# The second mixer's weight tiles are split during the first MLP and kept in DRAM as high and low parts

## The chip, the cores and the metric

The kernel runs on one core of a Trainium2 chip. The time is the device time of one execution in microseconds (us); lower is better. The engines are TensorE (PE, with PEld for its weight loads), VectorE (DVE), ScalarE (ACT), GpSimd (POOL) and SyncE (SP). SP and ScalarE each have a queue from which DMAs are issued.

## The reference

Two decoder layers on 528 tokens (16 meta tokens and 512 of input), width 1024, all in float32:

```python
for l in range(DEPTH):                       # DEPTH = 2
    a = rmsnorm(h, mix_pre_g[l])
    proj = a @ w_in[l]                       # 1024 x 2304: q, k, v, b_gate, c_gate, hc
    q, k = partial_rope(q, cos, sin), partial_rope(k, cos, sin)
    y_attn = sliding_window_gqa_sinks(q, k, v, sinks[l])
    y_conv = short_gated_conv(b_gate, c_gate, hc, conv_w[l])
    y = concat(rmsnorm(y_attn, ...), rmsnorm(y_conv, ...))
    h = h + rmsnorm(y @ w_out[l], mix_post_g[l])
    a = rmsnorm(h, mlp_pre_g[l])
    f = square(relu(a @ w_up[l])) @ w_down[l]   # 1024 -> 4096 -> 1024
    h = h + rmsnorm(f, mlp_post_g[l])
return h[:, N_META:]
```

## The kernel before

Activations stand transposed: 128 partitions of the feature dimension, 8 blocks `k`, 528 tokens in two ranges (272 and 256). Each float32 operand is split into a high part, rounded to `F32R`, and a low part, the rest. A product is three matmuls, hi·hi, hi·lo and lo·hi (`mm3`, lines 195 to 198), so a gemm of one weight tile (1024 x 128) with one range is 8 x 3 = 24 matmuls into one of eight PSUM banks.

A weight tile is loaded in two halves of 128 x 512 into `wraw` (five buffers) by SP's queue. `cast` (line 106) splits a half: ScalarE writes the high part (line 107), VectorE subtracts it from the raw half (line 108). `blocks` (line 80) lists all weight tiles in the order in which they are used: for each layer the two tiles of k and v, four of q, twelve of the gates and the convolution's input, eight of `w_out`, then in four chunks the tiles of `w_up` and `w_down`. `prep` (line 134) loads and splits the next block into two tiles of the tag `w`, which has 14 slots: seven tiles ahead (`CAP`), five in part of the mixer (`PCAP`). `tile_done` frees a tile after its last gemm and prepares the next. In chunks 1 to 3 the up projections run in pairs of tiles (`fast_pair`) with seven products in place of eight; their sums of weight blocks (lines 123 to 130) are made by VectorE.

The Mixer (`mixer`) projects, swaps halves for rope by four small DMAs per range and tile (lines 558 and 559, to rows of `z`), and runs attention in 128-token blocks between the gemms: scores (line 653), softmax (line 629), transposes (line 684) and the product with v (line 202). Sums of squares for the norms are taken by a matmul with a matrix of ones (line 235). `boundary` ends a sub-layer: norms and residual for the first range stand beside the last gemms of the second, then `first_tiles` runs the first five tiles of the next sub-layer.

The MLP (`mlp`) takes chunk after chunk: eight up tiles, then eight down tiles; `one` runs one tile's gemms over both ranges. In chunk 0 five up tiles run in `first_tiles` and three through `one`, and in the last chunk two down tiles go through `one` and six are shared with `boundary`.

The instructions are issued by a scheduler when the program is built: it puts each engine's instructions into a fixed order, taking what is ready by its own model of time, in the program's order where several are. On the chip each engine follows its order and waits on semaphores.

Of the kernel before, what the change touches and what calls it, by code (L numbers as in the profile page):

```python
# [8 lines left out]
F32 = mybir.dt.float32  # L9
F32R = mybir.dt.float32r  # L10
# [3 lines left out]
P = 128  # L14
# [22 lines left out]
def trunk_kernel(ctx, tc, xT, gains, sinkb, sinkm, rope, masks, maskm, ident_in, w_in, w_out, w_up, w_down, outT):  # L37
    nc = tc.nc
    ACT, DVE, POOL, PE = nc.scalar, nc.vector, nc.gpsimd, nc.tensor
# [3 lines left out]
    cp = ctx.enter_context(tc.tile_pool(name="cp", bufs=1))  # L43
# [33 lines left out]

    epst = cp.tile([P, 4], F32, name="epst")

    blocks = []  # L80
    for l in range(2):
        blocks += [("in", l, 512), ("in", l, 640)]
# [13 lines left out]
    prepared = []  # L96
    last_load = []
# [5 lines left out]
    def half():  # L103
        return wp.tile([P, 4, P], F32, tag="wraw", name="wraw", bufs=5)

    def cast(raw, hi, lo):
        ACT.activation(hi, raw, AF.Copy)  # L107
        DVE.tensor_tensor(lo, raw, hi.bitcast(F32), ALU.subtract)  # L108
# [4 lines left out]
    def prep_pair(l, m, n):  # L113

        if n == 0:
            for name, k, mm in (("A11", 0, m), ("A21", 0, m + 1), ("A22", 4, m + 1), ("A12", 4, m)):
                pair[name] = half()
                nc.sync.dma_start(pair[name], w_up[l].rearrange("(k p) m -> p k m", p=P)[:, k:k + 4, P * mm:P * mm + P])
        flat = lambda t: t.rearrange("p k m -> p (k m)")
        f = wp.tile([P, KT, P], F32R, tag="w", name="wf", bufs=2 * CAP)  # L120
        if n == 1:
            pair["S1"], pair["S2"] = (utile()[:, :512].rearrange("p (k m) -> p k m", k=4) for _ in range(2))
            DVE.tensor_tensor(pair["S1"], pair["A21"], pair["A22"], ALU.add)
            DVE.tensor_tensor(pair["S2"], pair["A11"], pair["S1"], ALU.subtract)
        if n == 2:
            pair["S3"] = pair["A21"]
            DVE.tensor_tensor(pair["S3"], pair["A21"], pair["A11"], ALU.subtract)
        if n == 6:
            pair["S4"] = pair["S2"]
            DVE.tensor_tensor(pair["S4"], pair["A12"], pair["S2"], ALU.add)  # L130
        cast(pair[("A11", "S2", "S3", "S1", "A12", "A22", "S4")[n]], f[:, 0:4, :], f[:, 4:8, :])
        prepared.append((f[:, 0:4, :], f[:, 4:8, :]))

    def prep(beside=None):

        if len(prepared) == len(blocks):
            return
        taken[0] += size(len(prepared))
        kind, l, sub = blocks[len(prepared)]
        if kind == "upx":  # L140
            return prep_pair(l, *sub)
        hi = wp.tile([P, KT, P], F32R, tag="w", name="whi", bufs=2 * CAP)
        lo = wp.tile([P, KT, P], F32R, tag="w", name="wlo", bufs=2 * CAP)
        raws = []
        for i in range(2):
            raw = half()
            raws.append(raw)
            ks = slice(4 * i, 4 * i + 4)
            dma = nc.sync.dma_start
            if kind == "out":  # L150
                col = slice(P * sub, P * sub + P)
                if i == 0:
                    for g in range(2):
                        dma(raw[g * 64:(g + 1) * 64], w_out[l, g * 256:(g + 1) * 256, col].rearrange("(j p) m -> p j m", p=64))
                else:
                    dma(raw, w_out[l, 512:1024, col].rearrange("(k p) m -> p k m", p=P))
            elif kind == "q":
                for g in range(2):
                    last_load[:] = [dma(raw[:, :, 64 * g:64 * g + 64], w_in[l].rearrange("(k p) m -> p k m", p=P)[
                        :, ks, 256 * g + 64 * sub:256 * g + 64 * sub + 64])]  # L160
            elif kind == "down":
                c, m = sub
                dma(raw, w_down[l, c * 1024:(c + 1) * 1024, P * m:P * m + P].rearrange("(k p) m -> p k m", p=P)[:, ks, :])
            else:
                src, off = (w_in, sub) if kind == "in" else (w_up, P * sub)
                last_load[:] = [dma(raw, src[l].rearrange("(k p) m -> p k m", p=P)[:, ks, off:off + P])]
            if beside:

                beside[2 * i]()
                cast(raw, hi[:, ks, :], lo[:, ks, :])  # L170
                beside[2 * i + 1]()
        if not beside:
            for i in range(2):
                ks = slice(4 * i, 4 * i + 4)
                cast(raws[i], hi[:, ks, :], lo[:, ks, :])
        prepared.append((hi, lo))

    def wtile():
        used[0] += 1
        return used[0] - 1  # L180

    def wtiles(n):
        return [wtile() for _ in range(n)]

    def refill(most=9):
        while len(prepared) < len(blocks) and taken[0] + size(len(prepared)) <= 2 * cap[0] and most:
            prep()
            most -= 1

    def tile_done(most=9):  # L190
        taken[0] -= size(done[0])
        done[0] += 1
        refill(most)
# [10 lines left out]
    def mms(items, act, hooks={}):  # L204


        banks = [bank() for _ in items]
        items = [(prepared[w], r, ev) for w, r, ev in items]
        for k in range(KT):
            ahi, alo = act(k)  # L210
            for (w, (t0, t1), _), ps in zip(items, banks):
                mm3(ps[:, :t1 - t0], w[0][:, k, :], w[1][:, k, :], ahi[:, t0:t1], alo[:, t0:t1], k == 0, k == KT - 1)
            if k in hooks:
                hooks[k]()
        return [lambda ev=ev, ps=ps, n=t1 - t0: ev(ps[:, :n]) for (_, (t0, t1), ev), ps in zip(items, banks)]

    def gemm(item, act):
        for ev in mms([item], act):
            ev()
# [47 lines left out]
    def new_acc(name):  # L267
        accs[name] = tp.tile([P, L], F32, tag="acc", name="acc", bufs=2)
        held.discard(name)
# [228 lines left out]
    def xrange(l):  # L498
        return (RA if l == 0 else XA, RB)
# [395 lines left out]
    def f_evac(m, r):  # L895
        t0, t1 = r

        def ev(ps):
            f = tmp(t1 - t0) if t1 - t0 <= 272 else utile()[:, :t1 - t0]
            DVE.tensor_scalar(f, ps, 0.0, None, ALU.max)  # L900
            ACT.activation(f, f, AF.Square)
            split(f_hi[:, m, t0:t1], f_lo[:, m, t0:t1], f)
        return ev
# [80 lines left out]
    def mlp(l, nxt, first):  # L984

        xr = xrange(l)

        full = xr if l == 0 else [(xr[0][0], xr[1][1])]

        def one(evac, act):  # L990
            w = wtile()
            for r in full:
                gemm((w, r, evac(r)), act)
            tile_done()

        txs[l] = [wp.tile([P, 4, L // 2], F32R, tag="x", name="tx", bufs=3) for _ in range(3)]
        for c in range(NCH):
            if c == 0:
                for m in range(NA, 8):
                    one(lambda r: f_evac(m, r), act_a)  # L1000
            else:
                for m in range(0, 8, 2):
                    fast_pair(l, m)
            last = c == NCH - 1
            if last:
                new_acc("h")
            for m in range(2 if last else 8):
                one(lambda r: z_evac(m, r, c > 0, last, (l, G_MPOST)), act_f)
                if c == 0 and m < 4:
                    fast_sums(l, m)  # L1010
        if nxt is not None:
            clear_pad()
        w = wtiles(6)
        for m in range(6):
            gemm((w[m], xr[0], z_evac(2 + m, xr[0], True, True, (l, G_MPOST))), act_f)
        boundary(l, w, act_f, G_MPOST, lambda r: Post(l, G_MPOST, r, nxt), first)

    def clear_pad():
        POOL.memset(kk[:, :, :PAD].bitcast(F32), 0.0)

    m0, m1 = Mixer(0), Mixer(1)
    first = [(m.items, m.tables, PCAP, "c") for m in (m0, m1)]
    sA, sB = Start(0, 0, RA, (0, 0)), Start(0, 0, RB, (0, 0))
    prep((lambda: sA.load(0), lambda: sA.steps(0), lambda: sA.load(1), lambda: sA.steps(1)))
    prep((lambda: sA.load(2), lambda: sA.steps(2), lambda: sA.load(3), lambda: sA.steps(3)))
    for i in range(4):
        prep()
# [12 lines left out]
    first_tiles(act_a, sB, RA, RB, first[0])  # L1040
    mixer(0, m0, mlp_items(0))
    mlp(0, (1, G_PRE), first[1])
    mixer(1, m1, mlp_items(1))
    mlp(1, None, None)


# [57 lines left out]
```

## Time and profile before

| | us |
|---|---|
| median of 3 runs | 1097.63 (1096.83 to 1098.42) |
| the profiled execution | 1097.51 |
| its span, first to last instruction | 1095.7 |
| TensorE busy | 1074.3 |
| VectorE busy | 801.3 |
| ScalarE busy | 624.6 |
| bytes read from and written to HBM | 97.88 MB, 2.10 MB |

In the profile a group of instructions is named by line, engine, operation and tile (`wlo<-wraw,whi` writes wlo from wraw and whi). The granted clock of TensorE was 0.996 over the span. In the profiled execution the first mixer runs up to about 200 us, the first MLP from 214 to 540 us, the boundary and the second mixer from 540 to about 750 us, and the second MLP from there to the end.

### The profile page before, as it was taken

The page shows a single profiled execution, that of the slowest core. Times are in us where ns is not written, and L with a number is a line of the kernel's source. Part 1 is how long each engine was busy: PE and PEld are TensorE (multiplying, and loading weights), DVE is VectorE, ACT ScalarE, POOL GpSimd, SP SyncE. Part 2 cuts the span into 40 slices and gives each one's busy share as a digit, 9 for nine tenths or more (in the row PEclk, how much of TensorE's full clock was granted, in tenths as well). Part 3 has the DMA queues.
Part 4 walks back from the last instruction along what each step waited for, and adds up shares of the span by engine and source line. Part 5 has one row for each costly group of instructions (what it writes and reads, how often), then busy time and mean ns, then how long its engine had stood idle before and what let it go on. Part 6 is the DMA issues. An engine that isn't in the chain of part 4 may idle for free.

```text
span 1095.7 us, 21642 instructions
## 1 busy us (share of the span) xinstructions
PE 1074.3 (98%) x8196; PEld 1030.8 (94%) x8196; DVE 801.3 (73%) x1895; ACT 624.6 (57%) x1510; POOL 10.8 (1%) x44
## 2 busy tenths in 40 slices
PE   8999999999999999999999999999999999999995
PEld 8999999999999999999989999999889989989995
DVE  7797886977585586586597988779947757757735
ACT  7576766665472383275365676667636625725732
POOL 2000000000000000000000000000000000000000
PEclk9999999999999999999999999999999999999998
DMA  9252122252252243144141412232422522522402
GB/s 249 64 146 59 58 78 79 77 155 59 69 152 85 59 127 110 49 124 137 26 112 39 130 58 59 78 97 82 130 72 84 154 68 79 162 68 71 143 1 77
DMA packets 206057, 102.06 MB, mean 93 GB/s; under 512 B 24000, under 2 KB 205904, under 8 KB 205952
## 3 DMA queue, kind: packets, MB, share of 16 engines
q1 hardware_dynamic: 205088, 99.89, 31.9%
q8 instruction: 64, 1.05, 0.4%
q10 hardware_dynamic: 688, 0.58, 0.2%
q14 instruction: 41, 0.34, 0.1%
q0 software_dynamic: 176, 0.21, 0.1%
HBM read 97.88 MB, written 2.10 MB: 91 GB/s over the span
## 4 chain that ended last, share of the span: by engine, by line
PE 88%; DVE 7%; ACT 1%; DMA 1%; issue 1%; SPq 1%; DVEq 0%; ACTq 0%
PE ps L196 28%; PE ps L198 28%; PE ps L197 28%; PE ps L202 1%; PE ps L684 1%; PE ps L653 1%; DVE wlo L108 1%; DVE a_lo L338 1%; DVE h L327 1%; DVE acc L280 1%; PE ps L235 1%; DMA h<-in_xT 0%; DVE t L326 0%; DMA z<-t 0%; SPq L558 0%
## 5 line engine op out<-in xcount | busy, mean ns | idle before, releaser
L197 PE MATMUL ps<-f_lo,whi 128*128 128x256 f32 (+2 forms) x1072 | 326.1, 305 | 0.0
L198 PE MATMUL ps<-f_hi,wlo 128*128 128x256 f32 (+2 forms) x1072 | 325.5, 305 | 0.0
L196 PE MATMUL ps<-f_hi,whi 128*128 128x256 f32 (+2 forms) x1072 | 322.9, 306 | 0.0
L197 PE MATMUL ps<-a_lo,whi 128*128 128x256 f32 (+3 forms) x808 | 230.2, 289 | 2.0 <-DVE a_lo L338 1.7
L196 PE MATMUL ps<-a_hi,whi 128*128 128x256 f32 (+3 forms) x808 | 227.2, 294 | 4.8 <-ACT a_hi L380 1.9
L198 PE MATMUL ps<-a_hi,wlo 128*128 128x256 f32 (+3 forms) x808 | 229.2, 288 | 0.1
L108 DVE TENSOR_TENSOR wlo<-wraw,whi 128x512 fp32r<-128x512 f32 x264 | 174.2, 688 | 51.8 <-ACT whi L107 31.5
L198 PEld LDWEIGHTS ps<-f_hi,wlo 128*128 128x128 f32 x1072 | 202.1, 189 | 9.1
L197 PEld LDWEIGHTS ps<-f_lo,whi 128*128 128x128 f32 x1072 | 201.6, 188 | 9.5
L107 ACT ACTIVATE whi<-wraw 128x512 fp32r<-128x512 f32 x264 | 153.9, 624 | 95.4 <-PE ps L197 58.4
L196 PEld LDWEIGHTS ps<-f_hi,whi 128*128 128x128 f32 x1072 | 199.5, 188 | 9.4
L196 PEld LDWEIGHTS ps<-a_hi,whi 128*128 128x128 f32 x808 | 148.1, 189 | 9.9 <-ACT a_hi L380 2.3
L197 PEld LDWEIGHTS ps<-a_lo,whi 128*128 128x128 f32 x808 | 152.6, 189 | 5.0 <-DVE a_lo L338 2.6
L198 PEld LDWEIGHTS ps<-a_hi,wlo 128*128 128x128 f32 x808 | 152.9, 189 | 1.4 <-DVE wlo L108 0.3
L510 DVE TENSOR_TENSOR z<-z,ps 128x272 f32<-128x272 f32 (+2 forms) x78 | 38.0, 487 | 99.9 <-PE ps L198 99.8
L107 ACT ACTIVATE wf<-wraw 128x512 fp32r<-128x512 f32 x96 | 59.7, 626 | 85.4 <-PE ps L197 51.8
L197 PE MATMUL ps<-a_lo,wf 128*128 128x264 f32 (+1 forms) x384 | 108.0, 282 | 0.0
L196 PE MATMUL ps<-a_hi,wf 128*128 128x264 f32 (+1 forms) x384 | 107.8, 282 | 0.0
L198 PE MATMUL ps<-a_hi,wf 128*128 128x264 f32 (+1 forms) x384 | 107.1, 283 | 0.0
L107 ACT ACTIVATE wf<-u 128x512 fp32r<-128x512 f32 x72 | 45.1, 627 | 88.4 <-PE ps L197 73.6
L108 DVE TENSOR_TENSOR wf<-wraw,wf 128x512 fp32r<-128x512 f32 x96 | 65.7, 688 | 11.5 <-ACT wf L107 10.5
L197 PEld LDWEIGHTS ps<-a_lo,wf 128*128 128x128 f32 x384 | 72.2, 188 | 0.1
(158 smaller groups left out, 1776.5 us busy)
## 6 DMA issues: line engine op xcount, KB each, us to landing
wraw<-in_w_up SPq DMA_DIRECT2D x128, 256.0 KB
wraw<-in_w_down SPq DMA_DIRECT2D x128, 256.0 KB
wraw<-in_w_in SPq DMA_DIRECT2D x56, 256.0 KB
wraw<-in_w_in SPq DMA_DIRECT2D x32, 128.0 KB
wraw<-in_w_out SPq DMA_DIRECT2D x32, 128.0 KB
wraw<-in_w_out SPq DMA_DIRECT2D x16, 256.0 KB
h<-in_xT SPq DMA_DIRECT2D x4, 272.0 KB
h<-in_xT SPq DMA_DIRECT2D x4, 256.0 KB
```

Source lines behind the costliest of these rows:

```text
L107: ACT.activation(hi, raw, AF.Copy)
L108: DVE.tensor_tensor(lo, raw, hi.bitcast(F32), ALU.subtract)
L196: PE.matmul(ps, whi, ahi, start=first, stop=False, skip_group_check=onto)
L197: PE.matmul(ps, whi, alo, start=False, stop=False, skip_group_check=onto)
L198: PE.matmul(ps, wlo, ahi, start=False, stop=last, skip_group_check=onto)
L202: PE.matmul(ps, a[n], b[n], start=first and n == 0, stop=last and n == 1)
L235: PE.matmul(ps, ones[:, which, :], acc, start=True, stop=more is None)
L280: return (eng or DVE).tensor_tensor(acc, acc, sq, ALU.add)
L327: DVE.tensor_tensor(hk, hk, t, ALU.add)
L338: DVE.scalar_tensor_tensor(a_lo[:, k, t0:t1], hk, g, a_hi[:, k, t0:t1].bitcast(F32), ALU.mult, ALU.subtract)
L510: DVE.tensor_tensor(zz, zz, ps, ALU.add)
L653: PE.matmul(outs[g], q[a][rows], k[b][rows], start=n == 0, stop=n == 2)
```

## The change

Two tiles are added, `sr` (a raw half) and `sf` (its high and low part), with one buffer each, and a pool `dp` in DRAM. In the first MLP, `one` calls `stash` after each gemm. A stash splits the half in `sr` into `sf`, stores `sf` to a DRAM tile of its own (128 x 2 x 512 words) and loads the next raw half into `sr`; both DMAs are issued on ScalarE's queue. `to_stash` has the 52 halves of the second layer's 26 tiles of `w_in` and `w_out`. `one` runs 29 tiles with two gemms each in the first MLP (three up, 26 down), so there are 58 calls, of which 52 do something. For a tile that is in `stashed`, `prep` issues four loads on SP's queue from DRAM straight into `hi` and `lo`; it uses no `wraw` and no `cast`. The loads of raw halves are moved into a function, `load_half`, unchanged.

```diff
+    sr = cp.tile([P, 4, P], F32, name="sr")
+    sf = cp.tile([P, 2, 4, P], F32R, name="sf")
+    dp = ctx.enter_context(tc.tile_pool(name="dp", bufs=1, space=bass.MemoryType.DRAM))
...
+    stashed = {}
+    to_stash = [(b, i) for b in blocks if b[1] == 1 and b[0] in ("in", "q", "out") for i in range(2)]
+
+    def stash():
+        if not to_stash:
+            return
+        (kind, l, sub), i = to_stash.pop(0)
+        cast(sr, sf[:, 0], sf[:, 1])
+        t = dp.tile([P, 2, 4, P], F32R, name=f"st_{kind}_{sub}_{i}")
+        ACT.dma_start(t.bitcast(F32), sf.bitcast(F32))
+        stashed.setdefault((kind, l, sub), []).append(t)
+        stash_load()
+
+    def stash_load():
+        if to_stash:
+            block, i = to_stash[0]
+            load_half(ACT, sr, *block, i)
...
     def prep(beside=None):
...
+        if (kind, l, sub) in stashed:
+            src = stashed[(kind, l, sub)]
+            for n, t in enumerate((hi, lo)):
+                for i in range(2):
+                    nc.sync.dma_start(t[:, 4 * i:4 * i + 4, :].bitcast(F32), src[i][:, n].bitcast(F32))
+            prepared.append((hi, lo))
+            return
...
             for r in full:
                 gemm((w, r, evac(r)), act)
+                if l == 0:
+                    stash()
             tile_done()
 
+        if l == 0:
+            stash_load()
         txs[l] = [wp.tile([P, 4, L // 2], F32R, tag="x", name="tx", bufs=3) for _ in range(3)]
```

More of the change, by code (lines that the diff above doesn't have):

```diff
@@ L132, in prep_pair, with load_half @@
         prepared.append((f[:, 0:4, :], f[:, 4:8, :]))
+    def load_half(queue, raw, kind, l, sub, i):
+        ks = slice(4 * i, 4 * i + 4)
+        dma = queue.dma_start
+        if kind == "out":
+            col = slice(P * sub, P * sub + P)
+            if i == 0:
+                for g in range(2):
+                    dma(raw[g * 64:(g + 1) * 64], w_out[l, g * 256:(g + 1) * 256, col].rearrange("(j p) m -> p j m", p=64))
+            else:
+                dma(raw, w_out[l, 512:1024, col].rearrange("(k p) m -> p k m", p=P))
+        elif kind == "q":
+            for g in range(2):
+                last_load[:] = [dma(raw[:, :, 64 * g:64 * g + 64], w_in[l].rearrange("(k p) m -> p k m", p=P)[
+                    :, ks, 256 * g + 64 * sub:256 * g + 64 * sub + 64])]
+        elif kind == "down":
+            c, m = sub
+            dma(raw, w_down[l, c * 1024:(c + 1) * 1024, P * m:P * m + P].rearrange("(k p) m -> p k m", p=P)[:, ks, :])
+        else:
+            src, off = (w_in, sub) if kind == "in" else (w_up, P * sub)
+            last_load[:] = [dma(raw, src[l].rearrange("(k p) m -> p k m", p=P)[:, ks, off:off + P])]
+    stashed = {}
[13 more added lines that the diff above has]
+            load_half(ACT, sr, *block, i)
     def prep(beside=None):
@@ L148, in prep @@
             ks = slice(4 * i, 4 * i + 4)
[L149 to L166, printed above, removed]
+            load_half(nc.sync, raw, kind, l, sub, i)
             if beside:
```

## Prediction

> **What bounds the kernel now.** I read the page first: its span, the busy times, the chain that ended last and the two costliest groups that the change touches.
>
> ```profile
> span 1095.7 us, 21642 instructions
> PE 1074.3 (98%) x8196; PEld 1030.8 (94%) x8196; DVE 801.3 (73%) x1895; ACT 624.6 (57%) x1510; POOL 10.8 (1%) x44
> ...
> PE 88%; DVE 7%; ACT 1%; DMA 1%; issue 1%; SPq 1%; DVEq 0%; ACTq 0%
> ...
> L108 DVE TENSOR_TENSOR wlo<-wraw,whi 128x512 fp32r<-128x512 f32 x264 | 174.2, 688 | 51.8 <-ACT whi L107 31.5
> ...
> L107 ACT ACTIVATE whi<-wraw 128x512 fp32r<-128x512 f32 x264 | 153.9, 624 | 95.4 <-PE ps L197 58.4
> ```
>
> TensorE is the bound nearly everywhere: 98% busy and 88% of the chain. Splitting half a weight tile costs 624 ns on ScalarE (hi) and 688 ns on VectorE (lo). VectorE holds 7% of the chain, so it matters in some stage; the table by stretches says which. Its columns are busy time and count of PE, PEld, DVE, ACT, POOL, then the clock, the DMA share and GB/s. The first four rows are the first MLP, the boundary into the second mixer, that mixer's start and its rest; then come a stretch of the up projections in pairs, one of down projections and the first 20 us; the last five rows are the same table for line 108 and for line 107 alone.
>
> ```profile
> 214.00:540.00 326.00, 325.22 (x2669) 324.89 (x2669) 219.92 (x447) 169.84 (x383) 1.43 (x4) 1.00 0.33 95
> 540.00:580.00 40.00, 37.70 (x294) 35.90 (x292) 36.01 (x91) 24.32 (x60) 1.92 (x6) 1.00 0.33 88
> 580.00:632.00 52.00, 49.00 (x416) 46.93 (x414) 44.39 (x146) 31.63 (x91) 0.46 (x4) 1.00 0.32 89
> 632.00:760.00 128.00, 127.29 (x1072) 125.32 (x1071) 105.12 (x284) 85.46 (x224) 0.00 (x0) 1.00 0.26 75
> ...
> 291.00:332.00 41.00, 41.00 (x340) 41.00 (x339) 34.13 (x72) 31.58 (x73) 0.00 (x0) 1.00 0.47 135
> 332.00:378.00 46.00, 46.00 (x380) 46.00 (x379) 24.55 (x44) 10.71 (x20) 0.00 (x0) 1.00 0.21 62
> ...
> 0.00:20.00 20.00, 16.67 (x95) 15.23 (x96) 13.00 (x28) 14.52 (x33) 6.55 (x26) 0.91 0.95 249
> ...
> 540.00:580.00 40.00, 6.65 (x11) 1.00 0.33 88
> 580.00:632.00 52.00, 10.39 (x16) 1.00 0.32 89
> ...
> 214.00:540.00 326.00, 91.74 (x154) 1.00 0.33 95
> 540.00:580.00 40.00, 6.38 (x12) 1.00 0.33 88
> 580.00:632.00 52.00, 8.96 (x15) 1.00 0.32 89
> ```
>
> In the first MLP TensorE never stops (325.2 of 326 us) while VectorE has a third of its time free and ScalarE half. From 540 to 632 us VectorE is at 36.0 of 40 and 44.4 of 52, and TensorE loses time: in the down stretch 380 matmuls took 46 us, 0.121 us each, so 40 us would hold 331 and held 294: 37 x 0.121 = 4.5 us lost. From 580 to 632, with its shorter matmuls, the idle time alone is 3.0 us. So what can be won lies between 540 and 632 and is about 7.5 us. Which waits are these? The waits of TensorE:
>
> ```profile
> PE ps L196 <- DVE vv L284: 1.5, 1, 1.5
> PE ps L196 <- ACT acc L301: 1.3, 1, 1.3
> PE ps L202 <- ACT p L283: 1.2, 1, 1.2
> ...
> PE ps L235 <- DVE acc L280: 1.0, 1, 1.0
> ...
> PE ps L684 <- DVE S L638: 0.3, 1, 0.3
> ```
>
> and the chain through the same stretch (start, us, what):
>
> ```profile
> 550.34 1.21 DVE wlo L108 x2
> ...
> 555.46 0.68 DVE wlo L108
> ...
> 560.30 0.26 DVE wlo L108
> ...
> 561.38 0.71 PE ps L235 x2
> ...
> 608.65 3.28 DMA wraw<-in_w_in
> ...
> 617.24 1.28 DVE wlo L108 x2
> 618.60 1.20 DVE wlo L108 x2
> ...
> 622.03 1.20 DVE wlo L108 x2
> ...
> 631.10 0.61 ACT p L283
> ```
>
> Two of the five waits end chains with weight splits in them: the matmul at 561.4 (line 235) and those at 626.6 and 631.7 (lines 684, 202).
>
> **The change, part by part.** (a) *Removed.* The 26 tiles of the second mixer are 52 halves. In the boundary and the mixer's start 27 splits leave VectorE (6.65 + 10.39 = 17.0 us) and ScalarE (6.38 + 8.96 = 15.3 us). At line 235 the 1.0 us goes, with about 0.2 us of slowed matmuls. At lines 202 and 684, 1.2 + 0.3 = 1.5 us goes: splits and their late load stand on the way there. The other slowed matmuls are 4.5 + 3.0 less the five waits (5.3), 2.2 us; I take 0.9, since they go with VectorE's load. The line 301 wait (1.3) follows a chain from 561.38 without a split, the line 284 wait (1.5) follows SP's queue (d): I take nothing, since no split stands before them. Sum of the gain 3.6; bounds 0 (latency takes the splits' place) and 7.5 (all lost time).
>
> (b) *Added work in the first MLP.* Each of 52 stashes is one 624 ns activation, one 688 ns subtraction, one store (512 KB) and one load (256 KB), both issued on ScalarE's queue. The nearest issue on that queue, and the nearest load and its user:
>
> ```profile
> 1089.99 2.79 ACTq L356 DMA_DIRECT2D outT<-h  x2
> ...
> 291.55 2.86 SPq L118 DMA_DIRECT2D wraw<-in_w_up  x2
> ...
> 297.03 0.69 DVE L123 TENSOR_TENSOR u<-wraw 128x512 f32<-128x512 f32 x1 [1.13 <-DMA wraw<-in_w_up]
> ```
>
> An issue is between 0.34 and 0.62 us (the rows in d); I take 0.4. VectorE gets 52 x 0.688 = 35.8, so 255.7 of 326 us; ScalarE 52 x (0.624 + 0.8) = 74, so 244 of 326. Both fit. What hides it: tiles are prepared seven ahead, a free third of VectorE, and eight PSUM banks. It is not even, though. The pair stretch has ScalarE at 31.6 of 41 and VectorE at 34.1 of 41. A stash asked for every gemm (24 x 0.121 = 2.9 us) cannot be done that fast: sr and sf have one buffer, so a turn is activation, subtraction, two issues and the landing. The load above was issued at 291.55 + 2.86 - 0.37 = 294.0 and used at 297.03: 3.0 us; in a burst 3.3 (the chain's 608.65 row). So a turn is at least 0.62 + 0.69 + 0.8 + 3.0 = 5.1 us. Its upper bound: the first 20 us moved 249 GB/s with the engines 95% busy, so 262 at most, and 768 KB take 3.0 us of transfer; added whole, 8.1. I take 5.5, near the single load, since the engines are two thirds free there. Then 52 turns are 286 us and end near 500: they spill from the down stretches into the pair stretches, 7.5 turns in each, +10.7 us on ScalarE (42 of 41) and +5.2 on VectorE (39 of 41). Weight splits may slip there, covered by the tiles ahead; without that cover each of three passages from pairs to downs waits one stash (1.3 us), 3.9 us. I take 0.4 and keep 0 to 3.9.
>
> The Trainium skill, "DMA: Bandwidth & Descriptors", section on the anatomy of one DMA, says that a DMA's semaphore cannot fire before its last byte is confirmed in the target memory, and that HBM is the heaviest target; its fit (2.0 us plus the bytes at 436 GB/s) would give an estimate of 3.2 us for a 512 KB store. By that the turn would be 5.3 us and the sum the same; no run so far shows a 512 KB store.
>
> (c) *Bytes.* Stores add 27.3 MB and raw reads 13.6 MB to the first MLP. At 262 GB/s that is 156 us of all engines over 326: the share goes from 0.33 to at most 0.81. In the mixer each tile is read as 1 MB in place of 512 KB, its 0.26 to 0.33 going to about 0.5. Loads are asked for tiles ahead, so I take 0; without the cover, a load is late by the transfer of one store, 2 us, once per passage, less than (b)'s bound.
>
> (d) *SP's queue.* Input tiles other than q take four loads in place of two, output tiles four in place of three: 14 x 2 + 8 = 36 more issues, many of them near the mixer's start, where SP has no gap:
>
> ```profile
> 549.25 0.34 SPq L539 DMA_DIRECT2D z<-in_rope  x1
> ...
> 578.94 0.71 SPq L558 DMA_DIRECT2D z<-t  x1
> ...
> 607.98 0.62 SPq L559 DMA_DIRECT2D z<-t  x1
> 608.65 2.64 SPq L166 DMA_DIRECT2D wraw<-in_w_in  x5
> ```
>
> Forty rope swaps run from 578.94 to 608.6 with three loads among them; five loads follow, 0.53 us each. Eight more issues ahead of the swaps would cost 8 x 0.53 = 4.2 us; behind them, nothing. The five loads stand behind, so I take 0. A load now also waits for its tile's slot, freed by TensorE, with swaps queued behind it; slots come free five tiles ahead in the mixer (29 us at 5.8 us a tile), which covers it.
>
> Sum: -3.6 + 0.4 = -3.2 us. The profiled execution took 1097.5 us, 1.8 beyond its span and 0.1 under the median of 1097.6. **Predicted: 1094.4 us.** About 0.2% (2.2 us) is what a measurement here can tell from no change.
>
> **The rivals.** *The stash loop is slower than the order allows (slower).* The order on each engine is fixed before the run. If it puts the next activation 5.0 us after the last and the chip's turn is 5.5, ScalarE stands at it 0.5 us each time, with the evacuations and weight splits of the first MLP queued behind; nothing gives the delay back, since the loop runs back to back, and at each passage from pairs to downs TensorE waits for the last f tiles. It decides from a difference of 0.06 us a turn (52 x 0.06 = 3.2). The wait of 1.13 us in line 123's row, before a load that the order took for landed, speaks for it; against it, such DMA waits are rare in this stage. A price of 0.35 us a turn gives 18 us: 1094 + 18 = 1112. The Trainium skill's rule above is on this side: the store's receipt is in every turn.
>
> *ScalarE is full in the pair stretches (slower).* At 42 of 41 us the passages wait; 3.9 us, and as much again for slipped splits: 1094 + 7.4 = 1101.
>
> *The gain stays out (no change).* The boundary is a latency chain and SP's queue the limit after it; line 235 alone is won, or SP's 4.2 us take the rest: 1097.
>
> **How the numbers follow.** Forecast 0.42; late loop 0.30; full ScalarE 0.10; no change 0.18. So faster 0.42, same 0.18, slower 0.40. The forecast's own range is 1090 (all 7.5 us won) to 1095.4. The whole range is 1090 to 1116: above it lies the loop that is late by over 0.4 us a turn, about 0.13, and below it 0.05.
>
> **What would show it.** In the profile after: splits of lines 107 and 108 gone between 540 and 632 us; the line 235 and line 202 waits gone; VectorE under 30 of 40 us at the boundary. In the first MLP TensorE should still be at 325 of 326 us. If that stage is longer, with ScalarE waiting for a DMA at the activation into sf, the late loop is right; if ScalarE is over 40 of 41 us in pair stretches and TensorE waits for f there, the second rival. If the stage is unchanged and the waits move to rope swaps, the third.

## The result and the profile after

The changed kernel takes 1141.31 us (median of 4 runs, 1139.65 to 1142.56) against 1097.23 for the kernel before (4 runs): a ratio of 1.040, 95% interval 1.0382 to 1.0418. It is 44 us slower where 3.2 us faster was forecast, and 25 us above the top of the range. The profiled execution took 1140.69.

Line numbers are those of the new file: `cast` is at 113 (ScalarE) and 114 (VectorE), `mm3` at 232 to 234, the stash's store at 171; the rows of an experiment have the line numbers of its own kernel. First the page: span, busy times, the chain that ended last, and bytes.

```profile
span 1138.9 us, 21877 instructions
...
PE 1090.0 (96%) x8196; PEld 1039.9 (91%) x8196; DVE 803.4 (71%) x1895; ACT 625.7 (55%) x1510; POOL 10.7 (1%) x44
...
HBM read 125.14 MB, written 29.36 MB: 136 GB/s over the span
...
PE 70%; DMA 13%; DVE 7%; ACT 6%; issue 2%; SPq 1%; ACTq 1%; DVEq 0%
PE ps L232 22%; PE ps L234 22%; PE ps L233 22%; DMA sr<-in_w_in 7%; DMA sr<-in_w_out 2%; PE ps L238 1%; ACT whi L113 1%; DMA wraw<-in_w_in 1%; ACT sf L113 1%; PE ps L689 1%; PE ps L720 1%; DVE wlo L114 1%; ACT S L665 1%; DVE sf L114 1%; DVE acc L316 1%
```

VectorE and ScalarE do the same number of instructions as before (1895 and 1510) in nearly the same busy time, and TensorE does the same 8196 matmuls. Of the 43 us of span that came on top, TensorE is idle for 27.5; it is busy 15.7 us longer, at a mean granted clock of 0.984 where it had 0.996. So the loss is waiting, and slower matmuls in its wake (the last section has one such stall). TensorE's share of the chain fell from 88% to 70%, and the raw loads of the stash, `sr<-in_w_in` and `sr<-in_w_out`, hold 9% of it.

Next the table by stretches, cut where the same work stands: first mixer, first MLP, boundary, start of the second mixer (before: 0 to 214, 214 to 540, 540 to 580, 580 to 632). The first row is that of the first mixer before, then come the four of after.

```profile
0.00:214.00 214.00, 210.67 (x1700) 205.53 (x1701) 174.10 (x490) 141.71 (x375) 6.95 (x30) 0.99 0.37 104
...
0.00:244.00 244.00, 219.81 (x1704) 210.27 (x1704) 192.21 (x521) 159.45 (x407) 6.93 (x30) 0.97 0.67 191
244.00:580.00 336.00, 328.96 (x2659) 326.19 (x2660) 228.86 (x462) 177.13 (x400) 1.43 (x4) 0.99 0.49 144
580.00:619.00 39.00, 37.66 (x298) 36.26 (x297) 29.99 (x80) 18.73 (x48) 1.91 (x6) 1.00 0.50 161
619.00:675.00 56.00, 51.94 (x417) 49.56 (x415) 37.62 (x132) 24.04 (x78) 0.40 (x4) 0.94 0.52 171
```

The first mixer takes 30 us longer, the first MLP 10, the boundary 1 less, the mixer's start 4 more. The first mixer is a stage that the prediction did not name at all. Why it pays is in the answer for line 113, with the row of the activation into `sf` (durations in ns, then first and last start) and what ended ScalarE's idle time before that line (us, times):

```profile
L113 ACT ACTIVATE sf<-sr x52: 614/632/716, 6.6 to 382.5; 128x512 fp32r<-128x512 f32 x52
...
  DMA sr<-in_w_in: 29.6, 21
  DMA sr<-in_w_out: 26.3, 16
```

And in TensorE's waits (us in total, times, longest):

```profile
PE ps L238 <- ACT p L319: 13.1, 3, 10.2
PE ps L232 <- ACT whi L113: 4.3, 1, 4.3
PE ps L233 <- DVE a_lo L374: 4.2, 6, 1.1
```

The stash runs from 6.6 to 382.5 us: it starts with the program, although `one` is called only in the first MLP. Nothing it reads comes from the first MLP, so the scheduler took it when it was ready. A turn is (382.5 - 6.6) / 51 = 7.4 us, and ScalarE stands at the activation into `sf` for a transfer 37 times, 56 us in all. Its mixer work stands behind: TensorE waits 10.2 us once for the scores' `p`, and 4.3 once for `whi`. Before the wait for `p`, ScalarE has these rows:

```profile
82.76 0.63 ACT L113 ACTIVATE sf<-sr 128x512 fp32r<-128x512 f32 x1 [2.02 <-DMA sr<-in_w_in]
83.30 0.40 ACT L665 ACTIVATE S<-S,ng 128x144 f32<-128x144 f32 x1
...
90.98 1.05 ACT L319 ACTIVATE p<-ps 128x512 fp32r<-128x512 f32 x2
```

A whole softmax (line 665) stands behind the activation that waits for the transfer, and `p` behind the softmax. The 2.0 us at that activation are only a part of the 10.2: the order of ScalarE and VectorE there is another than before, and what each part is worth no run separates.

The stall behind `whi`, on ScalarE's timeline (start, us, what; in brackets the idle time before and its releaser); the last row is SP's:

```profile
18.07 0.40 ACT L315 ACTIVATE t<-h 128x256 f32<-128x256 f32 x1
23.12 0.34 ACTq L171 DMA_DIRECT2D st_in<-sf  x1
23.50 0.45 ACTq L159 DMA_DIRECT2D sr<-in_w_in  x1
24.00 0.63 ACT L113 ACTIVATE whi<-wraw 128x512 fp32r<-128x512 f32 x1 [5.53 <-DMA z<-in_rope]
...
18.01 0.50 SPq L576 DMA_DIRECT2D z<-in_rope  x1
```

The table by stretches around it:

```profile
16.00:20.00 4.00, 4.00 (x33) 3.92 (x32) 2.42 (x5) 2.47 (x6) 0.00 (x0) 1.00 1.26 267
20.00:24.00 4.00, 0.36 (x3) 0.14 (x2) 0.00 (x0) 0.00 (x1) 0.00 (x0) 1.00 1.04 245
24.00:28.00 4.00, 3.32 (x13) 3.10 (x14) 3.24 (x7) 3.97 (x10) 0.00 (x0) 0.58 1.04 300
```

The stash's second store is issued at 23.12 and everything behind it on ScalarE waits, 5.5 us in all; what the issue itself waits for is in the last section. From 20.4 to 24 us TensorE, VectorE and ScalarE all stand still; after that the granted clock is 0.58 for 4 us.

To follow where time is lost I use TensorE's lateness: the start of its n-th main matmul less that in the kernel before, from the two traces, at times of the kernel before. Here it is +6.5 us at 30, +18.5 at 92, +29.9 at 225, +40.5 at 344 and the same at 554; then +38.9 at 566 (1.6 won), +45.1 at 627, +42.9 at 690 and to the end.

The 4 us in the second mixer stand on SP's queue:

```profile
617.81 0.71 SPq L594 DMA_DIRECT2D z<-t  x1
...
628.88 0.86 SPq L194 DMA_DIRECT2D whi<-st_in  x2
629.84 0.38 SPq L194 DMA_DIRECT2D wlo<-st_in  x1
...
639.07 0.86 SPq L194 DMA_DIRECT2D whi<-st_in  x2
640.02 0.85 SPq L194 DMA_DIRECT2D wlo<-st_in  x2
...
650.44 0.62 SPq L595 DMA_DIRECT2D z<-t  x1
```

The rope swaps now take from 617.8 to 651.1 us (33.2) where they took 29.7: twelve loads, those of three tiles, stand among them where three loads stood.

### The profile page after: what moved, and what is told of

It reads as the page before. It is cut to its first block, busy times and chain, and to the rows that moved or that the text cites. A ratio compares the mean times of both kernels' runs of the same rounds, so it can differ in the third digit from the quotient of the medians.

```text
span 1138.9 us, 21877 instructions
## 1 busy us (share of the span) xinstructions
PE 1090.0 (96%) x8196; PEld 1039.9 (91%) x8196; DVE 803.4 (71%) x1895; ACT 625.7 (55%) x1510; POOL 10.7 (1%) x44
## 3 DMA queue, kind: packets, MB, share of 16 engines
HBM read 125.14 MB, written 29.36 MB: 136 GB/s over the span
## 4 chain that ended last, share of the span: by engine, by line
PE 70%; DMA 13%; DVE 7%; ACT 6%; issue 2%; SPq 1%; ACTq 1%; DVEq 0%
PE ps L232 22%; PE ps L234 22%; PE ps L233 22%; DMA sr<-in_w_in 7%; DMA sr<-in_w_out 2%; PE ps L238 1%; ACT whi L113 1%; DMA wraw<-in_w_in 1%; ACT sf L113 1%; PE ps L689 1%; PE ps L720 1%; DVE wlo L114 1%; ACT S L665 1%; DVE sf L114 1%; DVE acc L316 1%
## 5 line engine op out<-in xcount | busy, mean ns | idle before, releaser
L232 PE MATMUL ps<-a_hi,whi 128*128 128x256 f32 (+3 forms) x808 | 230.5, 299 | 11.3 <-ACT whi L113 4.3
L114 DVE TENSOR_TENSOR wlo<-wraw,whi 128x512 fp32r<-128x512 f32 x212 | 139.8, 687 | 51.2 <-ACT whi L113 29.1
L232 PEld LDWEIGHTS ps<-a_hi,whi 128*128 128x128 f32 x808 | 149.9, 191 | 18.5 <-ACT whi L113 4.8
L113 ACT ACTIVATE whi<-wraw 128x512 fp32r<-128x512 f32 x212 | 123.6, 623 | 77.3 <-PE ps L233 42.7
L113 ACT ACTIVATE wf<-u 128x512 fp32r<-128x512 f32 x72 | 45.1, 626 | 79.4 <-PE ps L233 66.6
L232 PEld LDWEIGHTS ps<-a_hi,wf 128*128 128x128 f32 x384 | 72.1, 188 | 3.0 <-ACT t L999 2.8
```

What stands on the lines that cost most here:

```text
L232: PE.matmul(ps, whi, ahi, start=first, stop=False, skip_group_check=onto)
```

## The experiments

Theory: ScalarE's fixed order now holds instructions that wait for the stash's transfers; what is queued behind them pays. Rivals: the reading side pays; the added splits have no room; the bytes or the issues pay. Letters of theories in an expectation are those of its own round of runs.

**The two sides apart.** e1 keeps the stash and lets the second mixer load and split as before; e2 stashes only the first tile, and all 26 tiles read it.

```diff
-        if (kind, l, sub) in stashed:                      # e1
+        if (kind, l, sub) in ():
```
```diff
-    to_stash = [... for i in range(2)]                     # e2
+    to_stash = [... for i in range(2)][:2]
-        if (kind, l, sub) in stashed:
-            src = stashed[(kind, l, sub)]
+        if l == 1 and kind in ("in", "q", "out"):
+            src = stashed[("in", 1, 512)]
```

> The stash runs as in the changed kernel, but the second mixer loads and splits its tiles as in the kernel before and never reads what was stored. In the changed kernel TensorE falls 40.5 us behind before 383 us, where the last stash ends, and 2.5 us more in the second mixer. Theory A (the stash is moved to the front, into the first mixer, and costs its time there): 1097.2 + 40.5 = about 1138 us, the last activation into sf near 383 us. Rival B (the reads back from DRAM are what costs): under 1110 us.

> Only the two halves of one tile are stashed, and all 26 tiles of the second mixer read those parts with four loads each, so the reading side stands alone; the numbers that it computes are not the reference's. Theory A: 1097.2 + 2.4 = 1099.6 us: about 1.7 us won up to the rope swaps (splits gone), about 4 us lost behind SP's queue, where loads stand among the swaps. Rival B: 1110 us or more. My prediction's term for the gain (3.6 us, SP's issues at nothing) would give 1093.6 us.

e1: 1137.69 us, 1.038 (1.0361 to 1.0399). e2: 1106.83, 1.0098 (1.0083 to 1.0113). The writing alone costs 41 us: lateness +31.5 at 225, +40.8 at 344, nothing after. In e2 the two stashes, still at the front of the program, cost 7.0 by 30 us and 6.1 from 92 us on; 1.6 is won at the boundary, and some 4.3 lost in the mixer. So e2 misses theory A's 1099.6 by the cost at the front, which that sum left out.

**Two loads a tile in place of four.** e3 is e2 with both halves of a part side by side in DRAM, so one load of 512 KB fills `hi` and one `lo`.

```diff
-                for i in range(2):
-                    nc.sync.dma_start(t[:, 4 * i:4 * i + 4, :].bitcast(F32), src[i][:, n].bitcast(F32))
+                nc.sync.dma_start(t.bitcast(F32), src[:, n].bitcast(F32))
```

> As the run with reads alone, but the high and the low part of a tile are each one load of 512 KB, so a tile is two issues on SP's queue in place of four (and in place of two to four before). If SP's issues among the swaps are what takes the gain back, this is 1092 to 1095 us and the scores' wait in the second mixer is gone; if the wait is for the bytes or the slots, it stays at 1099 to 1100 us.

1101.34 us, 1.0045 (1.003 to 1.006): 5.5 less than e2, and above the expected 1092 to 1095 by what the two stashes at the front cost (+5.5). Past them the reading side is now worth -2.8: 1.6 at the boundary, 1.3 in the mixer, where the scores' wait is gone. So the issues on SP's queue turned a gain of 2.8 us into a loss of 2.7.

**The stash held in the first MLP.** In e4 each stash, and the first load, is ordered behind ScalarE's newest ordinary weight split at that point of the program.

```diff
-                    stash()
+                    with tc.issue_after(pace[0].ins):      # pace[0]: the newest split of prep
+                        stash()
```

> The changed kernel with every stash's instructions ordered behind ScalarE's latest split of the ordinary weight tiles, so that they can't be moved ahead of the first MLP. Theory A (the place does it): TensorE loses at most 5 us in the first MLP, and with the 2.4 us of the reads the time is 1097 to 1105 us. Rival C (the loop with one buffer costs its waits for DMA wherever it stands, 56 us of ScalarE's waits in the changed kernel): 1115 to 1140 us, lost between 214 and 560 us.

1125.63 us, 1.0272 (1.0254 to 1.029). Its row of the activation into `sf`:

```profile
L113 ACT ACTIVATE sf<-sr x52: 615/632/634, 232.9 to 588.7; 128x512 fp32r<-128x512 f32 x52
```

Its waits:

```profile
ACT sf L113 <- DMA sr<-in_w_in: 52.8, 32, 3.9
ACT sf L113 <- DMA sr<-in_w_out: 29.9, 14, 3.7
...
PE ps L233 <- ACT f_hi L320: 4.1, 2, 3.0
```

The first mixer is whole again (+0.9 us at 225), so the place costs about 16 of the 44 us. The loop in its meant place still costs: +19.3 by 540, as rival C has it and not theory A (at most 5). A turn is (588.7 - 232.9) / 51 = 7.0 us, ScalarE waits for `sr` 46 times, 82.7 us in all, and the loop runs some 30 us past the MLP's last gemms (540 + 19 us) over the boundary that it was to relieve (+26.6 at 559).

Not every wait reaches TensorE. A pair stretch of e4 in the table by stretches:

```profile
291.00:332.00 41.00, 41.00 (x341) 41.00 (x340) 35.44 (x70) 30.54 (x70) 0.00 (x0) 1.00 0.76 212
```

From 254 to 354 us ScalarE waits for `sr` ten times, 15.2 us in all, with the DMA share at 0.73, and TensorE is busy for 100.0 of the 100 us. The loss comes in steps: 6.4 us by 247, behind the first turns, where TensorE waits 3.0 us for `f_hi`; then 12.0 between 347 and 540, and 7.2 more by 559, at the boundary.

**Reads alone, and half the tiles.** e5 is e3 with its two stashes held as in e4. e6 is e4 with two loads and 24 halves in place of 52.

```diff
-    to_stash = [... b[0] in ("in", "q", "out") for i in range(2)]      # e6
+    to_stash = [... (b[0] == "in" and b[2] >= 768) for i in range(2)]
```

> Reads alone with two loads a tile, and the one stashed tile's two halves held in the first MLP; the numbers computed are not the reference's. In the run with two loads TensorE was 5.5 us late by 30 us and won 2.8 us in the second mixer. If the two early stashes made the 5.5 us, this is 1096.7 - 2.8 = 1094 us (1093 to 1096) and TensorE is not late by 30 us; if the start is disturbed by something else, 1099 to 1102 us.

> Held in the first MLP, two loads a tile, and only the twelve tiles that are split between 552 and 634 us stashed (24 halves in place of 52). With the held run's turn of 6.8 us the stash ends near 233 + 24 x 6.8 = 397 us, clear of the boundary. Theory C (each turn costs ScalarE's wait for its load): 7.4 us lost in the first MLP, as the held run had lost by there, 2 us won by the reads: about 1102 us. Theory A alone (the boundary and the front are what hurts): 1095 to 1097 us.

e5: 1096.35 us (12 runs), 1.000 (0.9989 to 1.001); the two stashes cost 1.7 us, the reads give back 2.8, and TensorE is not late at 30 us. e6: 1107.63, 1.0097 (1.0081 to 1.0114), above both of its expected times: +10.7 us by 347 and up to the boundary, for 24 turns of 6.8 us, and with these twelve tiles the reads win nothing (+12.3 at the end).

**A second raw buffer.** e7 (24 halves) and e8 (52) load two turns ahead, with room from writing the low part over the raw half; the parts leave in two stores of 256 KB.

```diff
-        cast(sr, sf[:, 0], sf[:, 1])
+        sr = srs.pop(0)                                    # two buffers, loaded ahead
...
+        cast(sr, sf, sr.bitcast(F32R))
...
+        for n, part in enumerate((sf.bitcast(F32), sr)):
+            ACT.dma_start(stashed[...][:, n, 4 * i:4 * i + 4, :].bitcast(F32), part)
```

> The same 24 halves with the wait taken away: two buffers for the raw half, so that the next load is under way during a turn, and the low part written over the raw half; the high and the low part are two stores of 256 KB. Theory C: the wait of ScalarE for the raw half falls from 1.6 us a turn to under 0.5, the loss in the first MLP to 0 to 2 us, the time to 1094 to 1097 us. If what costs is the work itself on VectorE and ScalarE, or the bytes, the loss stays and the time is 1101 to 1104 us.

> All 52 halves with two buffers, low part in place, held in the first MLP, two loads a tile. A turn should be 4 to 5 us, so that the last stash is at 440 to 490 us, before the boundary. Theory C: 1094 to 1099 us. If the work itself costs, as much as in the held run inside the first MLP (13 us): 1106 to 1110 us.

e7: 1117.99 us, 1.0201 (1.0185 to 1.0217). e8: 1144.85, 1.0444 (1.0424 to 1.0463). Both miss either of their expected times: the loss went up, not down. Turns are shorter (5.5 and 5.7 us), yet ScalarE still waits. TensorE's waits in e8, over the run:

```profile
PE ps L237 <- ACT t L1004: 32.2, 6, 11.2
```

The first of the six lies between 291 and 303 us, in a pair stretch. ScalarE's waits there, then the table by stretches:

```profile
ACT sf L111 <- DMA sr<-in_w_in: 4.4, 2, 3.5
ACT wf L111 <- DMA st_in<-sr: 2.2, 1, 2.2
```

```profile
291.00:297.00 6.00, 4.93 (x41) 4.72 (x39) 2.03 (x4) 1.20 (x3) 0.00 (x0) 1.00 0.56 182
297.00:303.00 6.00, 2.94 (x13) 2.94 (x14) 3.71 (x7) 3.43 (x8) 0.00 (x0) 0.72 0.68 198
```

While TensorE waits 4.1 us for `t`, the pair's evacuation, ScalarE is busy 1.2 and 3.4 of 6 us: it is not full, it stands. Eight of the loop's splits fall into this pair stretch (291 to 332), where `wf` splits and evacuations stand right behind them. The lateness jumps in such stretches: +12.2 by 310, +33.5 by 407, +47.5 by 480. Ahead of the second jump ScalarE stands 6.8 us, up to 399.7, at an activation into `sf` that waits for the store of the one before it, as `sf` still has one buffer; TensorE then waits 10.5 us for `t`. Why such waits cost more here than in e4 no run separates. Past the MLP e8 wins 2.5, all 26 tiles read with two loads.

**Work without transfers.** e9 is e5 with 50 further splits of the same raw half, with no load and no store. e10 paces the loop of e7: one stash a tile (5.8 us), the first 24 halves. e11 is e6 with the stash's DMAs on SP's queue.

```diff
+            if more[0]:                                    # e9, where to_stash is empty
+                more[0] -= 1
+                cast(sr, sf[:, 0], sf[:, 1])
```
```diff
-                if l == 0:                                 # e10
+                if l == 0 and r is full[0]:
```
```diff
-        ACT.dma_start(stashed[...                          # e11; the loads too
+        nc.sync.dma_start(stashed[...
```

> The splits of the loop alone. Two halves are stashed with their stores and loads as in e5, all tiles of the second mixer read those two parts (two loads a tile, so the numbers are not the reference's), and 50 further times only the activation and the subtraction run, from the same raw half, held in the first MLP, with no store and no load. If ScalarE's waits for the loop's DMAs are the cost (theory W), the 50 splits cost next to nothing: 1096 to 1098, TensorE at +1 to +2 us at 542. If the work itself has no room on ScalarE (theory C), 50 x 0.62 = 31 us more of ScalarE bring at least half of what the held loop lost by 542 (19 us): 1106 or more.

> The first 24 halves (k, v, q and six more tiles) are stashed, one after the first gemm of each tile instead of after both, so at 5.8 us a tile and not at the loop's own speed, with two raw buffers and the low part written over the raw half, two loads a tile in the mixer. A turn has then 11.6 us for each raw buffer and should never wait for a DMA. Theory W: no lateness above 2 us at 542 and 1.5 to 2.5 us won behind it: 1094.5 to 1097, the first version that is not slower. Theory C: 24 activations and 72 issues of 0.35 to 0.6 us are 40 to 55 us of ScalarE, +8 us or more at 542: 1103 or more. If a single issue that waits for VectorE's subtraction or a transfer is enough (theory I), in between: 1098 to 1103.

> e6 (24 halves, one raw buffer, back to back, two loads a tile) with the loop's stores and loads issued on SP's queue instead of ScalarE's. If ScalarE is held by the issues that wait in its order for VectorE's subtraction and for the transfer before (theory I), this takes most of the loss away: 1097 to 1101. If it is held at the activation that waits for the raw half (theory W), the loss stays: 1105 to 1109, with the DMA waits at the activation into sf as before, and SP's own loads of weights may come later on top.

e9: 1099.1 us, 1.0026 (1.0016 to 1.0036), 1.1 above what theory W expects and far from theory C. Its group of the activations into `sf` (busy, mean ns, idle before and what ended it):

```profile
L113 ACT ACTIVATE sf<-sr 128x512 fp32r<-128x512 f32 x52 | 32.5, 625 | 30.1 <-DVE sf L114 21.4 <-DMA sr<-in_w_in 6.5 <-DMA st_in<-sf 2.1
```

Its first MLP in the table by stretches:

```profile
214.00:540.00 326.00, 323.04 (x2635) 322.38 (x2635) 246.57 (x491) 194.89 (x427) 1.43 (x4) 0.99 0.35 101
```

ScalarE did 25 us more there than before (169.84) and VectorE 27 us more. Lateness is +4.5 at 255, around the two real stashes and the activation that waits for their second store, and +4.5 at 530: from the fourth split on, nothing is lost. So the work is free where it stands here; what e9 leaves out, and what costs, is the transfers. It leaves out their bytes together with the waits for them: that it is the waits, the rows of e4, e8, e10 and e12 show. The scheduler put the splits into the down stretches (15, 16 and 13, against 2 and 1 in the pair stretches from 291 and 378), so a full ScalarE in pair stretches was not put to the test.

e10: 1102.59 us, 1.0052 (1.0037 to 1.0067), the least loss of any version that stores all that it reads, and where theory I, of an issue that waits, expects it. Three steps make it up: +2.2 by 247 (the first load), +1.1 by 296, +3.1 at 386. The last one on ScalarE's timeline:

```profile
378.37 0.44 ACTq L177 DMA_DIRECT2D st_in<-sr  x1
384.53 0.39 ACTq L158 DMA_DIRECT2D sr<-in_w_in  x1
384.97 0.63 ACT L111 ACTIVATE wf<-wraw 128x512 fp32r<-128x512 f32 x1 [8.68 <-PE ps L239]
```

The trace names TensorE for the 8.68 us, but the `wf` split starts 0.05 us behind the end of the issue at 384.53. That load overwrites a raw buffer, and goes 6.2 us behind the store from one that was issued last. So the issue holds ScalarE.

e11: 1109.85 us, 1.0123 (1.0109 to 1.0137): no gain over e6. The issues left ScalarE, the wait did not; ScalarE's waits:

```profile
ACT sf L113 <- DMA sr<-in_w_in: 72.3, 23, 6.1
```

The Trainium skill, "DMA: Bandwidth & Descriptors", section "Issuing engines are not separate DMA queues", says that DMAs run on the same DMA engines whichever engine issues them, and that issuing from several saves only the time of the issue; e11 against e6 (1.0123, 1.0097) agrees.

**Paced, and on SP's queue.** e12 is e10 with the DMAs on SP's queue and the first loads earlier.

```diff
-            with tc.issue_after(pace[0].ins):
+            with tc.issue_after(pace[-9].ins):             # pace now keeps the last 21 splits
                 stash_load()
```

> e10 with the loop's stores and loads issued on SP's queue, and its first two loads allowed some 25 us earlier, so that ScalarE holds no instruction that waits for a transfer and finds the raw half landed. In e10 ScalarE stood 8.7 us ahead of 384.97, behind the issue of a load at 384.53 whose buffer was still being stored; that cost TensorE 3 us. If the waits in ScalarE's order are all that is left of the loss (theory W), TensorE is less than 1 us late at 542 and what the boundary gave in e10 (1.6 us) stays: 1094.5 to 1096.5. If SP's queue, held by the same waits, brings weight loads late instead (theory Q), the loss moves there: 1099 or more, with DMA wraw among the waits of VectorE and ScalarE in the down stretches. If the work has no room after all (theory C): 1102 or more.

1103.79 us, 1.0065 (1.0052 to 1.0078); the time alone would fit theory Q and theory C, so the rows decide. TensorE is not late up to 303 us (-0.04), so neither the first load nor ScalarE's order costs anything there any more; then 5.9 us go within 4 us, in a pair stretch. SP's timeline ahead of it:

```profile
278.64 0.38 SPq L123 DMA_DIRECT2D wraw<-in_w_up  x1
279.12 0.51 SPq L177 DMA_DIRECT2D st_q<-sr  x1
283.45 0.92 SPq L151 DMA_DIRECT2D sr<-in_w_in  x2
284.47 0.45 SPq L177 DMA_DIRECT2D st_q<-sf  x1
285.01 0.38 SPq L123 DMA_DIRECT2D wraw<-in_w_up  x1
```

And VectorE's:

```profile
289.12 0.69 DVE L128 TENSOR_TENSOR u<-wraw 128x512 f32<-128x512 f32 x1 [5.70 <-DMA wraw<-in_w_up]
302.78 0.69 DVE L128 TENSOR_TENSOR u<-wraw 128x512 f32<-128x512 f32 x1 [4.78 <-DMA wraw<-in_w_up]
```

The weight load after the one of 278.64 is issued 6.4 us later, at 285.01: the stash load ahead of it goes 4.3 us behind the store of 279.12, whose raw buffer it may not overwrite sooner. VectorE stands 5.7 us for its raw half at 289.12 and 4.8 us at 302.78, and the pairs' splits with it; TensorE then waits 3.0 us for `t`. The wait moved from ScalarE's order to SP's, and the loss with it, as theory Q has it, though in a pair stretch and not in the down stretches.

## Why the prediction was wrong

*The place in (b) failed first.* The prediction took the calls in `one` for the time at which a stash runs (214 to 500 us) and read the cover from the first MLP's rows. The stash depends on nothing there, and the order is written by readiness; it ran from 6.6 us, in the mixer, which has no such cover. That costs about 16 us (1141.3 less 1125.6, after against e4).

*The cover in (b) failed second.* It counted what the added work needs against free shares. The work is indeed free (e9, in down stretches), but it needs a transfer each turn, and an instruction that waits for a transfer stops all that stands behind it in its engine's order, free share or not. What lies prepared ahead covers some of these waits (e4 from 254 to 354 us), not all. The forecast had the loss at 0.4 us, bound 3.9; it is 19 us in the first MLP (e4), more past it. The turn, taken at 5.5 (bounds 5.1 to 8.1), measures 7.0 to 7.4 with one buffer. The fit of the Trainium skill, "DMA: Bandwidth & Descriptors", section on the anatomy of one DMA, that gave the estimate of 3.2 us for a store and so a turn of 5.3, is stated there for DMAs issued from GpSimd. This loop's are issued on ScalarE's queue, and no run gives the time of one such store alone.

*The rival of the late loop* named this mechanism and its sign: "ScalarE waiting for a DMA at the activation into sf" is what the waits show. Its price did not hold: 0.35 us a turn was taken, ScalarE stands 56.0 / 52 = 1.1 us a turn, and TensorE loses 40.5 / 52 = 0.8, the case of over 0.4 that had a chance of 0.13. It too looked for the loss in the first MLP alone. (Its 52 x 0.06 is 3.1, not 3.2.)

*The rival of a full ScalarE* is not what happened: the changed kernel pays in the first mixer before it, and where pair stretches pay, ScalarE is not full: 30.7 of 41 us in after (324 to 365 us), half idle in e8.

*(a) was right in kind.* 1.6 us at the boundary (forecast 1.2 + a part of 0.9) and, with two loads a tile only, 1.3 in the mixer (e3): 2.8 of 3.6. In the changed kernel the wait of line 235 is gone, but the scores' wait of line 202, which was to go too, grew from 1.2 to 2.7 us; in e3 it is gone. (The prediction counts two waits behind weight splits and lists three; its sum takes all three.) VectorE is at 29.99 of 39 us in the boundary, as forecast under 30.

*(d) was mis-sized:* nothing taken, bound 4.2; four loads a tile cost 5.5 us more than two (e2 less e3), because loads stand among the swaps, not ahead or behind. That difference is 52 issues, where the change adds 36 to the kernel before, so it is more than the term itself; it eats more than (a), and the second mixer ends 4.0 us later.

*(c)* has the bytes right: 125.14 less 97.88 is 27.3 MB more read, and 29.36 less 2.10 is 27.3 MB more written. The DMA share is 0.67 in the first mixer, and 0.71 in the part of the first MLP in which the loop still runs (244 to 383 us), under the 0.81 allowed. e4 has 0.76 in a stretch in which TensorE loses nothing, so there the bytes cost nothing; what they add to the waits elsewhere no run separates.

Together: 40.5 us for the writing (29.9 by the end of the first mixer, the rest in the first MLP), -1.6 + 4.0 for the reading, 42.9 us. No version tried beats the kernel before; with the reading worth 2.8 us at best, the writing would have to cost less than that, and the least found is 6.7, with 24 of the 52 halves (e10).

## What to carry to other kernels

Where work is moved "beside" a stage, look for the dependence or the order that keeps it there; a call's place in the source is none. Price a moved step by its waits, not by its busy time: on an engine with a fixed order, each instruction or DMA issue that can wait for a transfer holds up everything behind it, and another queue only changes who pays (e12). Whether the last engine pays depends on what lies prepared ahead of it. A free share of an engine covers work of known length; a loop of load, split and store whose turns wait for each other's transfers has none, with one raw buffer or with two.

## What the runs showed of the hardware

A stall costs more than its length. After 4.3 us without matmuls (20.4 to 24.7 us) the granted clock was 0.58 from 24 to 28 us (one half from 24.65 to 28.06), and a wait of 4.3 us made TensorE 6.2 us late in all. The Trainium skill, "TensorE: Matmul & The Clock Gate", Part 1, puts the clock at half after an idle window of about 3.4 us, until about 3.4 us of work have passed; the trace agrees.

A DMA's issue can wait for a transfer that it shares no data with. The data of the store issued at 23.12 us were ready when VectorE's subtraction ended at 17.9. Just ahead of the issue, the trace has ScalarE's queue waiting for semaphore 101, on which the store will tell of its own landing; the last DMA to use it was the rope table's load that SP issued at 18.01, and its landing was told from 21.1 to 23.04. In this trace SP's and ScalarE's DMAs take turns on eight such semaphores, so ScalarE stood for a transfer of SP's queue. e1, e2 and e3 have the same stall, with the store's issue at 23.98, 23.73 and 22.91 us; it is most of what the two stashes at the front cost e2 and e3.
